# A decoder trunk in fp32 on one core: first weights of V split ahead of the scheduler, norm products two triples later, first output halves five blocks apart, late low weights by columns

## The chip, the cores and the metric

The kernel runs on one core of one Trainium2 chip. A core has TensorE (PE in the profile; its weight loads are listed as PEld), VectorE (DVE), ScalarE (ACT), GpSimd (POOL) and SyncE (SP, which here issues loads and stores). Each engine runs its own list of instructions in order, and waits by semaphores for the others. The metric is device time in microseconds (us) of one execution; lower is better.

## The reference

Two layers over 1024 positions of width 1024, all in fp32. The first is a gated delta rule with a gated FFN and was left as it is. The second is softmax attention over a band of keys, with a FFN behind it. The change lies between the end of the first FFN and the start of the second one:

```python
h = h + conv_ffn(rmsnorm(h, f_norm[0]), ...)              # layer 0 ends
kv = rmsnorm(h, kv_norm) @ w_kv                            # K and V, once
h = h + chunk_attention(rmsnorm(h, b_norm[0]), b_w_q[0], b_rel_bias[0], b_w_out[0], k_pad, v_pad)
# chunk_attention, for each chunk of 64 queries and each of 16 heads:
#   s = q . k * scale + bias          576 keys: own chunk and 8 before it
#   p = softmax(s);  o = p . v;       and at the end o @ w_out
h = h + conv_ffn(rmsnorm(h, f_norm[1]), ...)
```

## The kernel before

Every fp32 product is made of three matmuls of a faster type: an operand is split into a high part (a rounded copy: `whi`, `xh`, made on ACT) and a low part (the remainder: `wlo`, `xl`, made on POOL or DVE). `dense` (L114) then issues high × high (L120), high × low (L121) and low × high (L122). Three such matmuls, 128 × 128 by 128 × 512, are called a **block** here; the FFN's own form (L1395 to L1397) is called a triple. A tile of 128 output columns and all 1024 positions takes two halves `s` of 512 positions, each of 8 blocks, one for each 128 rows of the weights.

**End of the first FFN and the norm.** `part` (L1832) issues the triples of the last FFN product for half `s`, tile `m` and step `k`. At listed places it calls `next(norms[0])`, which runs the next piece of `norm_steps` (L351): squares on ACT, sums on DVE into `nacc` (L369), products with ones on PE (`pss`, L374), the root on ACT, then a broadcast by PE (`psb`, L387), from which DVE makes the normed activations (L392), ACT their high part (L395) and DVE or POOL their low part (L383).

**First tiles of K and Q.** `two_tiles` (L1337) runs one tile of K and one of Q, half by half. Their weights come by `load_w`, which folds the norm's gain in and splits (`split_w`, L91).

**Attention.** The eight pairs of heads `p` each need a tile of K, of Q and of V (`kv_tile`, L2004). From here a planner written in the kernel, `Flow` (L200), decides the order in which the code is emitted: it keeps a clock `T`, adds an assumed duration for all that it emits, holds a due time for each engine, and emits a dense block whenever nothing of higher rank is due. `Flow.fetch` prepares the next dense tile: a first step issues its load, a second splits its weights. If the tile at the front isn't split yet, `_dense` adds 3 us and more to the clock and then splits. Its order is fixed before the kernel runs. A tile of K or Q of pair `p` may start only when all scores of pair `p − 2` are out (`there`, key `scored`), because `kA` and `qA` have two buffers for each pair of tiles; one of V when the outputs of `p − 2` are.

For two heads and 256 queries at a time the attention goes as follows. PE writes scores to the one buffer `sc` (L2140, L2141). DVE adds the bias and takes the extreme into `sS` and `st` (L2145). ACT takes the exponential (L2149), DVE a reciprocal (L2153), POOL multiplies (L2155). PE transposes the result (`ptp`, L2200); ACT makes its high part `pTh` (L2213), DVE its low part `pTl` (L2220), and PE multiplies by V into `poT` (L2245, L2246). ACT and DVE fold that into `oT` (`tm` L2251, L2256). V itself is copied (`vt`, L2083), transposed on PE (`pvt`, L2064) and split into `V`.

**Output product.** `first_parts` (L2336) runs the first two tiles `m` of the output product over six of the eight weight rows, on activations made from `yo` (L2293 high, L2296 low). Its list `order` holds (m, s, k). `rest(s)` (L2381) adds the last two rows for half `s`, with weights in two pieces of 512 columns, and feeds the second FFN's norm.

Of the kernel before, what the change touches and what calls it, by code (L numbers as in the profile page):

```python
# [28 lines left out]
def trunk_kernel(  # L29
# [15 lines left out]
    nc = tc.nc  # L45
# [20 lines left out]
    g_kv = take(8)  # L66
    g_b = take(8)
# [334 lines left out]
    wv = None  # L402
# [107 lines left out]
    with ExitStack() as ph:  # L510
        wp = ph.enter_context(tc.tile_pool(name="wp0", bufs=2, **SB))
# [776 lines left out]
        wv = Flow()  # L1288
# [16 lines left out]
        with tc.manual_schedule(engines={mybir.EngineType.PE, mybir.EngineType.DVE, mybir.EngineType.Activation}):  # L1305
            tails = []
            acts, normed = [[[[None, None] for _ in range(KT)] for _ in range(2)] for _ in range(2)]
            for t in range(4):
                s, hds = heads(t)
# [24 lines left out]
            env["cut"] = 1  # L1334
            del env["run"]

    def two_tiles(wts, tail):  # L1337

        pss = [[pacc.tile([P, HALF], F32, name="acc", tag="u", bufs=4) for _ in range(2)] for _ in wts]
        for s in range(2):  # L1340
            for n, (ps, wt) in enumerate(zip(pss, wts)):
                for i in range(KT):
                    dense(ps[s], wt, 0, xh, xl, FULL[i : i + 1], s, first=i == 0, last=i == KT - 1)
                    if (n, i) in ((0, 6), (1, 3)):
                        next(tail, None)
            for _ in tail:
                pass
            yield pss
# [8 lines left out]
    def ffn(layer, h, hp, xs, tail, d_r, last):  # L1357
# [472 lines left out]
        if layer == 0:  # L1830

            def part(s, m, ks):  # L1832
                def f():
                    if ks[0] == 0:
                        if s == 0 and m > 3:
                            if m % 2 == 0:
                                fps["d"] = pacc.tile([P, SEQ], F32, name="pf", tag="d", bufs=2)
                            fps[s, m] = fps["d"][:, hs(m % 2)]
                        else:
                            fps[s, m] = pacc.tile([P, HALF], F32, name="pf", tag="u", bufs=4)  # L1840
                    for k in ks:
                        triple(fps[s, m], fw[m], [t_[:, hs(s)] for t_ in hid[k0 + k]], kc[k], k == 0, k == 3)
                        if (s, m, k) in ((1, 5, 1), (1, 6, 0)):
                            next(norms[0])
                return f

# [128 lines left out]
    ctx_o = ctx.enter_context(ExitStack())  # L1975
    wp = ctx_o.enter_context(tc.tile_pool(name="wp1", bufs=2, **SB))
    xh, xl = xb
    first = two_tiles([load_w(w_kv, 0, fold=g_kv, on_act=True), load_w(b_w_q, 0, fold=g_b, on_act=True)], tail0)
    next(first)
    ctx_f.close()  # L1980
    ctx_h.close()
# [2 lines left out]
    with ExitStack() as ph:  # L1984
# [18 lines left out]

        def kv_tile(src, c0, g, post):  # L2004

            shape = [P, KT, P]
            raw = wp.tile(shape, F32, name="wraw", tag="wraw", bufs=2)
            nc.sync.dma_start(out=raw, in_=src[:, c0 : c0 + P].rearrange("(k p) m -> p k m", p=P))
            yield
            wt = split_w(raw, shape, fold=g)  # L2010
            wv.on("G", 2.75, wv.on("A", 1.0, wv.on("G", 2.6)))
            yield
            for s in range(2):
                ps = pacc.tile([P, HALF], F32, name="acc", tag="acc", bufs=3)
                for i in range(KT):
                    dense(ps, wt, 0, xh, xl, FULL[i : i + 1], s, first=i == 0, last=i == KT - 1)
                    if i < KT - 1:
                        yield
                post(s, ps)
                yield  # L2020
# [291 lines left out]
        NO = 6  # L2312
# [23 lines left out]
        def first_parts():  # L2336
            raws = [part_raw(m) for m in range(2)]
            yield
            wts = [part_split(raws[0])]
            yield 20  # L2340
            wts.append(part_split(raws[1]))
            wv.brief = True
            order = [(0, 0, k) for k in range(3)]
            for k in range(3, NO):
                order += [(1, 0, k - 3), (0, 0, k)]
            order += [(1, 0, k) for k in range(NO - 3, NO)] + [(0, 1, k) for k in range(NO)]
            banks, done = {}, []
# [33 lines left out]
        def rest(s):  # L2381
            w_ = 1024 // (KT - NO)
            shape = [P, KT - NO, w_]
            raws, wts = [], []
            for c in range(KT - NO):
                raws.append(wp.tile(shape, F32, name="wraw", tag="wraw", bufs=2))
                nc.sync.dma_start(out=raws[c], in_=b_w_out[NO * P :, c * w_ : (c + 1) * w_].rearrange("(k p) m -> p k m", p=P))
            yield
            wts.append(split_w(raws[0], shape))
            wv.on("G", 2.7, wv.on("A", 1.0))  # L2390
            yield 11
            for m in range(KT):
                c = m * P // w_
                ps = pacc.tile([P, HALF], F32, name="acco", tag="acc", bufs=3)
                for k in range(NO, KT):
                    dense(ps, wts[c], m * P - c * w_, *acts, [(k - NO, k)], s, first=k == NO, last=k == KT - 1)
                    if k < KT - 1:
                        yield
                if m == 0:
                    wts.append(split_w(raws[1], shape))  # L2400
                    wv.on("G", 2.7, wv.on("A", 1.0))
# [19 lines left out]
                yield wv.T + (0.8, 2.2)[n] if n < 2 else wv.T + 1.1  # L2421

        queue_kv(0)
        wv.auto = False
        main_ps.close()
        pB = ph.enter_context(tc.tile_pool(name="pB", bufs=1, **PS))
        pacc = ph.enter_context(tc.tile_pool(name="paccB", bufs=1, **PS))
        env["cut"] = 4
        with tc.manual_schedule():
            for p in range(1, 8):  # L2430
                queue_kv(p)
            wv.add(1, "score", lambda: 0.0, score_run())
            wv.add(0.8, "turns", lambda: 0.0, turn_run())
            wv.add(0.6, "apply", lambda: 0.0, apply_run())
            for n, (s, k) in enumerate([(s, k) for s in range(2) for k in range(NO)]):
                wv.add(0.9, ("early", n % 6), wv.when(("d_o", k)), early_o(k, s))
            wv.add(0, "begin", wv.when(("o", 6), ("act", 6, 0), ("act", 6, 1)), begin())
            wv.dense.append((lambda: True, there(("act", 0, 0)), first_parts()))
            for m in range(2, KT):
                wv.dense.append((lambda: True, lambda: True, part(m, (0, 1) if m < 4 else (0,))))  # L2440
            for s in range(2):
                wv.dense.append((lambda: True, there(*[("act", k, s) for k in range(NO, KT)]), rest(s)))
                if s == 0:
                    for m in range(4, KT):
                        wv.dense.append((lambda: True, lambda: True, part(m, (1,))))
            wv.run(lambda: not (wv.dense or wv.items or wv.late or wv.cur or wv.nxt))
# [96 lines left out]
```

## Time and profile before

| | us |
|---|---|
| runs of the kernel, median (lowest to highest) | 2573.83 (2572.54 to 2575.70) |
| the profiled execution | 2573.15 |
| its span, first to last instruction | 2571.4 |
| first FFN ends, norm | about 1293 to 1340 |
| first tiles of K and Q | about 1340 to 1366 |
| attention | about 1366 to 1896, output product from 1775 |
| second FFN | from 1896 |

In the profile, a group's row gives the line, engine, operation, output and inputs by the program's names, and how many. Rows of the timeline begin with the start and the duration in us, and in brackets stands how long the engine was idle before and what released it. Rows of the waits give engine, tile and line, then what was waited for, and total us, times and longest us. Rows of the windows give for a stretch the length, the busy time of PE, PEld, DVE, ACT and POOL with the number of instructions in brackets, then the granted TensorE clock as a share of full speed, the busy share of the DMA engines and GB/s. L-numbers are lines of the kernel before.

### The profile page before, as it was taken

Reading aid. Unit: us, or ns where it says so; the run is one execution under the profiler, and the core shown is the slowest. Engines: PE = TensorE matmul, PEld = TensorE weight load, DVE = VectorE, ACT = ScalarE, POOL = GpSimd, SP = SyncE. Lnnn points to the kernel's source line nnn. Section 1 sums busy time; section 2 is a strip of 40 time slices with the busy share of each in tenths; the row PEclk is TensorE's granted clock in tenths of the full one; section 3 lists DMA queues with packets and bytes.
Section 4 is the critical chain, followed back from the end, with each engine's and each line's share of the span. In section 5 each row is a group of like instructions: output and inputs, shape, how many; then the busy total and the mean of one; then the engine's idle time right before and its main releaser. Section 6 shows DMA issues by size and latency. Waiting matters only on the chain. (4 is left out here: it accounts for less than half of the span.)

```text
span 2571.4 us, 39303 instructions
## 1 busy us (share of the span) xinstructions
PE 2506.2 (97%) x13957; PEld 2081.7 (81%) x13957; DVE 1824.8 (71%) x2956; ACT 1405.4 (55%) x2704; POOL 1484.8 (58%) x1511
## 2 busy tenths in 40 slices
PE   7999999999999999999999999999999999999998
PEld 5878788888777888888788888888877788888877
DVE  5765775454588888888866666666478788888885
ACT  6444555474456555565545555556455656555653
POOL 3655554245537777777725444445453777777770
PEclk9999999999999999999999999999999999999999
DMA  4534445455326676777841211122332467677785
GB/s 128 138 101 121 119 117 164 130 176 167 112 78 136 143 152 143 155 152 152 185 164 46 61 43 48 53 69 71 128 119 78 135 148 147 146 155 153 155 194 189
DMA packets 317061, 325.93 MB, mean 127 GB/s; under 512 B 32832, under 2 KB 240960, under 8 KB 316864
## 3 DMA queue, kind: packets, MB, share of 16 engines
q1 hardware_dynamic: 285728, 219.33, 28.7%
q0 software_dynamic: 26240, 95.43, 20.7%
q10 hardware_dynamic: 4896, 8.65, 1.0%
q8 instruction: 110, 1.80, 0.3%
q14 instruction: 87, 0.71, 0.1%
HBM read 180.68 MB, written 142.67 MB: 126 GB/s over the span
## 5 line engine op out<-in xcount | busy, mean ns | idle before, releaser
L1362 POOL TENSOR_TENSOR ul<-r,uh 128x512 fp32r<-128x512 f32 x276 | 438.3, 1607 | 276.1 <-ACT uh L1383 261.6
L105 POOL TENSOR_TENSOR wlo<-wraw,whi 128x256 fp32r<-128x256 f32 (+3 forms) x338 | 249.3, 768 | 227.1 <-ACT whi L103 192.4
L120 PE MATMUL acc<-xh,whi 128*128 128x512 f32 x896 | 377.8, 422 | 0.2
L122 PE MATMUL acc<-xh,wlo 128*128 128x512 f32 x896 | 354.9, 396 | 3.2 <-POOL wlo L105 3.2
L121 PE MATMUL acc<-xl,whi 128*128 128x512 f32 x896 | 355.1, 396 | 1.0 <-DVE xl L1102 0.6
L1383 ACT CAST uh<-r 128x512 fp32r<-128x512 f32 x290 | 178.2, 623 | 202.0 <-DVE r L1362 159.0
L1397 PE MATMUL pu<-xh,ul 128*128 128x512 f32 x528 | 207.1, 392 | 3.7 <-POOL ul L1362 3.7
L1395 PE MATMUL pu<-xh,uh 128*128 128x512 f32 x528 | 207.0, 392 | 2.9 <-POOL uh L1383 1.4
L1396 PE MATMUL pu<-xl,uh 128*128 128x512 f32 x528 | 206.5, 391 | 1.0 <-POOL xl L383 1.0
L122 PEld LDWEIGHTS acc<-xh,wlo 128*128 128x128 f32 x896 | 169.7, 189 | 41.4 <-POOL wlo L105 3.9
L1749 ACT COPY stage<-pd 128x1024 f32<-128x1024 f32 x180 | 174.9, 1013 | 50.3 <-PE pd L1397 49.4
L121 PEld LDWEIGHTS acc<-xl,whi 128*128 128x128 f32 x896 | 170.8, 191 | 27.3 <-DVE xl L1102 2.7
L120 PEld LDWEIGHTS acc<-xh,whi 128*128 128x128 f32 x896 | 170.7, 190 | 24.6 <-ACT xh L1101 1.1
L1490 DVE SCALAR_TENSOR_TENSOR gate<-gpre,colt,gate 128x1023 f32<-128x1023 f32 (+2 forms) x92 | 180.0, 1957 | 4.7 <-ACT gate L1487 3.8
L1362 POOL TENSOR_TENSOR dl<-a,dh 128x512 fp32r<-128x512 f32 x90 | 153.8, 1709 | 46.0 <-ACT dh L1383 46.0
L2155 POOL TENSOR_SCALAR sS<-sS,st 128x640 f32<-128x640 f32 (+4 forms) x128 | 85.7, 674 | 163.5 <-DVE st L2153 147.9
L1490 DVE SCALAR_TENSOR_TENSOR val<-vpre,colt,val 128x1023 f32<-128x1023 f32 x88 | 151.9, 1726 | 35.7 <-ACT val L1487 35.5
L2145 DVE CUSTOM_DVE_ANT_0 sS<-sc,bt 128x640 f32<-128x640 f32 (+4 forms) x128 | 84.1, 657 | 123.6 <-PE sc L2141 97.0
L1362 DVE TENSOR_TENSOR r<-r,r 128x512 f32<-128x512 f32 x160 | 126.4, 790 | 31.0 <-POOL ul L1362 29.6
L1397 PEld LDWEIGHTS pu<-xh,ul 128*128 128x128 f32 x528 | 99.5, 188 | 26.7 <-POOL ul L1362 6.2
L2213 ACT CAST pTh<-ptp 128x512 fp32r<-128x512 f32 (+2 forms) x176 | 76.1, 452 | 81.2 <-PE ptp L2200 79.6
L1395 PEld LDWEIGHTS pu<-xh,uh 128*128 128x128 f32 x528 | 99.4, 188 | 24.2 <-POOL uh L1383 1.9
(406 smaller groups left out, 7131.9 us busy)
## 6 DMA issues: line engine op xcount, KB each, us to landing
r<-in_f_w_up_dram SPq DMA_DIRECT2D x172, 256.0 KB, 4.3
d_r<-stage POOLq DMA_DIRECT2D x78, 512.0 KB, 7.7
d_c<-stage POOLq DMA_DIRECT2D x70, 512.0 KB, 7.8
a<-in_f_w_down_dram SPq DMA_DIRECT2D x72, 256.0 KB, 2.8
wraw<-in_a_w_in_dram SPq DMA_DIRECT2D x32, 512.0 KB, 4.7
d_e<-stage POOLq DMA_DIRECT2D x32, 512.0 KB, 8.8
wraw<-in_a_w_out_dram SPq DMA_DIRECT2D x16, 512.0 KB, 4.3
d_r<-h ACTq DMA_DIRECT2D x32, 256.0 KB, 3.4
```

The costliest lines, as they stand in the source:

```text
L105: nc.gpsimd.tensor_tensor(lo[:, c], raw[:, c], hi[:, c].bitcast(F32), op=ALU.subtract)
L120: mm(ps, hi[:, kw, wcol : wcol + P], rh[k][s], start=st, stop=False)
L121: mm(ps, hi[:, kw, wcol : wcol + P], rl[k][s], start=False, stop=False)
L122: mm(ps, lo[:, kw, wcol : wcol + P], rh[k][s], start=False, stop=sp)
L1362: tt = lambda eng, o, a, b, op: eng.tensor_tensor(o, a, b, op=op)
L1383: copy(hi, src)
L1395: mm(ps, w[0][:, cw], x[0], start=first, stop=False, skip_group_check=True)
L1396: mm(ps, w[0][:, cw], x[1], start=False, stop=False, skip_group_check=True)
L1397: mm(ps, w[1][:, cw], x[0], start=False, stop=last, skip_group_check=True)
L1490: nc.vector.scalar_tensor_tensor(t_[:, a:c1], p_[:, a - step : c1 - step], w[:, 2 - step : 3 - step], t_[:, a:c1], op0=ALU.mult, op1=ALU.add)
L1749: nc.scalar.copy(t_, ps)
L2155: nc.gpsimd.tensor_scalar(S, S, st[:, 3:4], 1.0, op0=ALU.mult, op1=ALU.mult)
```

## The change

1. In `two_tiles` a function `then` is called after K's second half. It issues the load and the split of V's first tile. `kv_tile` takes those weights if they are there. The next tile's load and split are asked for (`wv.fetch(0)`, `wv.fetch(2)`), and the first bias tiles are loaded, before the planner starts.
2. Two calls of the norm's steps move from the triples (1,5,1) and (1,6,0) to (1,5,3) and (1,6,2).
3. In `first_parts`, the first tile's half runs five blocks, not three, before the second tile's blocks alternate with it.
4. In `rest`, a weight piece's low part is made in four column groups of 128, over both its rows, instead of in one operation for each row.

```diff
-    def two_tiles(wts, tail):
+    def two_tiles(wts, tail, then):
...
+                if (s, n) == (1, 0):
+                    then()
...
-                        if (s, m, k) in ((1, 5, 1), (1, 6, 0)):
+                        if (s, m, k) in ((1,5,3),(1,6,2)):
                             next(norms[0])
...
+    ready = []
+
+    def next_tile():
+        raw = wp.tile([P, KT, P], F32, name="wraw", tag="wraw", bufs=2)
+        nc.sync.dma_start(out=raw, in_=w_kv[:, 1024 : 1024 + P].rearrange("(k p) m -> p k m", p=P))
+        ready.append(split_w(raw, [P, KT, P], fold=g_kv))
...
-            yield
-            wt = split_w(raw, shape, fold=g)
-            wv.on("G", 2.75, wv.on("A", 1.0, wv.on("G", 2.6)))
+            if ready:
+                wt = ready.pop()
+                yield
+            else:
...
-            order = [(0, 0, k) for k in range(3)]
-            for k in range(3, NO):
-                order += [(1, 0, k - 3), (0, 0, k)]
-            order += [(1, 0, k) for k in range(NO - 3, NO)] + [(0, 1, k) for k in range(NO)]
+            order = [(0, 0, k) for k in range(5)]
+            for k in range(5, NO):
+                order += [(1, 0, k - 5), (0, 0, k)]
+            order += [(1, 0, k) for k in range(NO - 5, NO)] + [(0, 1, k) for k in range(NO)]
...
+            def split(raw):
+                hi = wp.tile(shape, F32R, name="whi", tag="whi")
+                lo = wp.tile(shape, F32R, name="wlo", tag="wlo")
+                nc.scalar.copy(hi, raw)
+                for c in range(w_ // P):
+                    nc.gpsimd.tensor_tensor(lo[:, :, kc(c)], raw[:, :, kc(c)], hi[:, :, kc(c)].bitcast(F32), op=ALU.subtract)
...
         queue_kv(0)
+        wv.fetch(0)
+        wv.fetch(2)
...
         with tc.manual_schedule():
+            bias(0)
```

Since the planner's clock no longer stands at the opening, the order of the whole attention changes. Three places follow, first the opening of V's first tile on PE, before the change (`acc_13428` is V's first half, `sc` the scores):

```order
L120 MATMUL acc_13428<-xh0_0_13075,whi_13421 128x512
L121 MATMUL acc_13428<-xl0_0_13076,whi_13421 128x512
L122 MATMUL acc_13428<-xh0_0_13075,wlo_13422 128x512
L120 MATMUL acc_13428<-xh1_0_13077,whi_13421 128x512
L121 MATMUL acc_13428<-xl1_0_13078,whi_13421 128x512
L122 MATMUL acc_13428<-xh1_0_13077,wlo_13422 128x512
L2140 MATMUL sc_13446<-kA_13378,qA_13388 128x128
L2141 MATMUL sc_13446<-kA_13378,qL0_13390 128x128
```

After the change, all eight blocks of the first half (`acc_13436`) come first; these are the rows from its last block on:

```order
L120 MATMUL acc_13436<-xh7_0_13095,whi_13360 128x512
L121 MATMUL acc_13436<-xl7_0_13096,whi_13360 128x512
L122 MATMUL acc_13436<-xh7_0_13095,wlo_13361 128x512
L120 MATMUL acc_13467<-xh0_1_13241,whi_13360 128x512
L121 MATMUL acc_13467<-xl0_1_13242,whi_13360 128x512
L122 MATMUL acc_13467<-xh0_1_13241,wlo_13361 128x512
L2077 MATMUL pvt_13471<-ident_67,vt_13465 128x128 x4
...
L122 MATMUL acc_13467<-xh3_1_13247,wlo_13361 128x512
L2153 MATMUL sc_13501<-kA_13391,qA_13401 128x128
L2154 MATMUL sc_13501<-kA_13391,qL0_13403 128x128
```

So the first score stands behind 12 blocks of V where it stood behind two, and the first transposes of V (`pvt`) behind one block of the second half.

The second place is PE between V's fourth tile and K's fifth. Before (`acc_15416` is the end of that V tile, `acc_15530` that K tile):

```order
L122 MATMUL acc_15416<-xh7_1_13255,wlo_15203 128x512
L2200 MATMUL ptp_15510<-ident_67,sS_15289 128x128
L2200 MATMUL ptp_15510<-ident_67,sS_15342 128x128
...
L2245 MATMUL poT_15498<-pTh_15459,V_14718 128x256
L2246 MATMUL poT_15498<-pTl_15460,V_14718 128x256
...
L2064 MATMUL pvt_15523<-ident_67,vt_15506 128x128 x4
L120 MATMUL acc_15530<-xh0_0_13075,whi_15424 128x512
```

After, between the same two tiles (now `acc_15210` and `acc_15450`), one row for each group that stands there; a score has four such rows, a group of transposes two to four, a group of `poT` four:

```order
L122 MATMUL acc_15210<-xh7_1_13255,wlo_15062 128x512
...
L2077 MATMUL pvt_15325<-ident_67,vt_15305 128x128 x4
...
L2259 MATMUL poT_15333<-pTl_15322,V_14620 128x256
...
L2153 MATMUL sc_15350<-kA_14257,qA_14459 128x320
...
L2153 MATMUL sc_15370<-kA_14257,qA_14459 128x320
...
L2213 MATMUL ptp_15396<-ident_67,sS_15254 128x128
...
L2153 MATMUL sc_15405<-kA_14257,qA_14459 128x320
...
L2258 MATMUL poT_15413<-pTh_15363,V_14621 128x256
...
L2153 MATMUL sc_15426<-kA_14257,qA_14459 128x320
...
L2213 MATMUL ptp_15436<-ident_67,sS_15355 128x128
...
L2258 MATMUL poT_15444<-pTh_15391,V_14621 128x256
...
L120 MATMUL acc_15450<-xh0_0_13081,whi_15235 128x512
```

Where one group of transposes, one of `poT` and V's transposes stood, there are now four scores and the attention work between them, with no dense block.

The third place is the start of the output product on PE. Before, the second tile (`acco_18306`) follows the first (`acco_18272`) after three blocks:

```order
L122 MATMUL acco_18272<-xh2_0_18106,wlo_18149 128x512
L2200 MATMUL ptp_18297<-ident_67,sS_17950 128x128
L2200 MATMUL ptp_18297<-ident_67,sS_17994 128x128
...
L120 MATMUL acco_18306<-xh0_0_18102,whi_18265 128x512
L121 MATMUL acco_18306<-xl0_0_18103,whi_18265 128x512
L122 MATMUL acco_18306<-xh0_0_18102,wlo_18266 128x512
```

After, two more blocks and two scores with `poT` groups stand between the third block and the second tile (`acco_18294`):

```order
L122 MATMUL acco_18224<-xh2_0_18100,wlo_18113 128x512
L2077 MATMUL pvt_18243<-ident_67,vt_18196 128x128 x4
...
L122 MATMUL acco_18224<-xh3_0_18102,wlo_18113 128x512
...
L2153 MATMUL sc_18262<-kA_17592,qA_17857 128x128
...
L122 MATMUL acco_18224<-xh4_0_18104,wlo_18113 128x512
L2153 MATMUL sc_18282<-kA_17592,qA_17857 128x256
...
L122 MATMUL acco_18294<-xh0_0_18096,wlo_18218 128x512
```

On POOL the order at this place is the same in both, except that one product of scores (`sS`) moves ahead of the activations: three low parts of activations (`xl`), then the low part of the second weights.

More of the change, by code (lines that the diff above doesn't have):

```diff
@@ L1977, in trunk_kernel @@
     xh, xl = xb
-    first = two_tiles([load_w(w_kv, 0, fold=g_kv, on_act=True), load_w(b_w_q, 0, fold=g_b, on_act=True)], tail0)
+    ready = []
[3 more added lines that the diff above has]
+        ready.append(split_w(raw, [P, KT, P], fold=g_kv))
+    first = two_tiles([load_w(w_kv, 0, fold=g_kv, on_act=True), load_w(b_w_q, 0, fold=g_b, on_act=True)], tail0, next_tile)
     next(first)
@@ L2004, in kv_tile @@
         def kv_tile(src, c0, g, post):
-            shape = [P, KT, P]
-            raw = wp.tile(shape, F32, name="wraw", tag="wraw", bufs=2)
-            nc.sync.dma_start(out=raw, in_=src[:, c0 : c0 + P].rearrange("(k p) m -> p k m", p=P))
-            yield
-            wt = split_w(raw, shape, fold=g)
-            wv.on("G", 2.75, wv.on("A", 1.0, wv.on("G", 2.6)))
+            if ready:
+                wt = ready.pop()
+                yield
+            else:
+                shape = [P, KT, P]
+                raw = wp.tile(shape, F32, name="wraw", tag="wraw", bufs=2)
+                nc.sync.dma_start(out=raw, in_=src[:, c0 : c0 + P].rearrange("(k p) m -> p k m", p=P))
+                yield
+                wt = split_w(raw, shape, fold=g)
+                wv.on("G", 2.75, wv.on("A", 1.0, wv.on("G", 2.6)))
             yield
@@ L2388, in rest @@
             yield
-            wts.append(split_w(raws[0], shape))
-            wv.on("G", 2.7, wv.on("A", 1.0))
+            def split(raw):
[4 more added lines that the diff above has]
+                    nc.gpsimd.tensor_tensor(lo[:, :, kc(c)], raw[:, :, kc(c)], hi[:, :, kc(c)].bitcast(F32), op=ALU.subtract)
+                wv.on("G", 2.9, wv.on("A", 1.0))
+                wts.append((hi, lo))
+            kc = lambda c: slice(c * P, (c + 1) * P)
+            split(raws[0])
             yield 11
@@ L2399, in rest @@
                 if m == 0:
-                    wts.append(split_w(raws[1], shape))
-                    wv.on("G", 2.7, wv.on("A", 1.0))
+                    split(raws[1])
                 nc.vector.tensor_tensor(h[m][:, hs(s)], ps, h[m][:, hs(s)], op=ALU.add)
```

## The prediction

> **What bounds the kernel now.** I read the page first, for the share of each engine.
>
> ```profile
> span 2571.4 us, 39303 instructions
> PE 2506.2 (97%) x13957; PEld 2081.7 (81%) x13957; DVE 1824.8 (71%) x2956; ACT 1405.4 (55%) x2704; POOL 1484.8 (58%) x1511
> ```
>
> TensorE (PE) is the bound: in a span of 2571.4 us it has no matmul under way for only 65 us. No edit here removes a matmul, so the change can only touch those 65 us, and the speed at which matmuls run. Next I read the table of waits, which names what ended each idle time of PE. These are its rows on the code that the diff touches, or whose order it can move:
>
> ```profile
> PE acco L122 <- POOL wlo L105: 2.7, 3, 1.9
> PE sc L2140 <- DVE qL L2051: 2.3, 1, 2.3
> PE pvt L2064 <- ACT vt L2083: 0.9, 4, 0.3
> PE sc L2140 <- DVE st L2145: 0.8, 1, 0.8
> PE pss L374 <- DVE nacc L369: 0.6, 1, 0.6
> ```
>
> Together 7.3 us, 0.28% of the span. Then I read busy time and granted clock in short stretches, because the two longest of these waits are followed by something that the table doesn't show:
>
> ```profile
> 1370.00:1373.00 3.00, 3.00 (x11) 2.34 (x10) 0.73 (x4) 1.09 (x4) 0.00 (x0) 0.55 0.86 273
> 1373.00:1376.00 3.00, 3.00 (x14) 2.51 (x13) 0.71 (x4) 0.71 (x2) 0.83 (x2) 0.88 0.00 0
> 1780.00:1783.00 3.00, 3.00 (x12) 2.64 (x12) 1.78 (x4) 1.88 (x5) 3.00 (x6) 0.50 0.53 156
> 1783.00:1786.00 3.00, 3.00 (x14) 2.44 (x13) 0.37 (x2) 0.00 (x0) 3.00 (x3) 0.94 0.88 296
> 1893.00:1900.00 7.00, 4.43 (x19) 3.05 (x18) 6.69 (x10) 4.05 (x7) 6.27 (x5) 1.00 0.89 285
> ```
>
> The number behind POOL's busy time is the granted clock. It is 0.55 and then 0.88 behind the wait that ends at 1369.6, and 0.50 and then 0.94 behind the one that ends at 1779.8. PE counts as busy there, but does less. Lost in the first pair: 3 × 0.45 + 3 × 0.12 = 1.7 us; in the second: 3 × 0.50 + 3 × 0.06 = 1.7 us. In the last row PE is idle for 2.6 of 7 us and the clock stays 1.00, so idle time alone doesn't decide it.
>
> **Weights of V in front of the scheduler, first wait.** In the before, only two blocks of V's tile stand ahead of the first score, which waits for the low part of the query tile:
>
> ```profile
> 1366.90 0.40 PE L122 MATMUL acc<-xh,wlo 128*128 128x512 f32 x1
> 1368.07 1.39 DVE L2051 SCALAR_TENSOR_TENSOR qL<-acc,qA 64x512 fp32r<-64x512 f32 x2
> 1369.61 0.30 PE L2140 MATMUL sc<-kA,qA 128*128 128x128 f32 x1 [2.31 <-DVE qL L2051]
> ```
>
> After the change 12 blocks stand ahead of it (order of the change: 8 of the first half, 4 of the second). A block is three matmuls, and matmuls of 512 columns start 0.23 us apart though each is recorded with 0.39 or 0.40 (1882.50 and 1882.73 below); so a block is 0.68 us, and a recorded wait costs 0.16 us more than it says. The ten added blocks last 6.8 us, far more than the 2.31 us. Gain: 2.31 + 0.16 + 1.7 of clock = **4.2 us**; at least 2.5, if the clock drops there for another reason. Those blocks are brought forward, not added: they are missing later, which is the last term of the sum. V's casts and subtractions move ahead of the last casts of K and Q on ACT and POOL, and the load of the next K tile moves behind two bias loads on SP's queue; all three have some 6 us of V blocks more in front of them than before. The one new price: V's first transposes (pvt) now come one block after the copy they need. The row above has four such waits, 0.9 us together; a fifth is 0.2 + 0.16, about **0.4 us** lost (0 to 0.5).
>
> **Norm's products two triples later.**
>
> ```profile
> 1330.29 0.39 PE L1397 MATMUL pf<-hidh,fl 128*128 128x512 f32 x1
> 1331.30 1.05 PE L374 MATMUL pss<-ones,nacc 128*128 128x2 f32 x8 [0.63 <-DVE nacc L369]
> 1337.53 0.69 DVE L1362 TENSOR_TENSOR h<-pf,h 128x512 f32<-128x512 f32 x1 [1.31 <-PE pf L1397]
> ```
>
> Two triples are 1.4 us of matmuls put in front of a wait of 0.63. Gain 0.63 + 0.16 = **0.8 us**. The products themselves start 0.6 us later than now, and with them the root, the reciprocal and the broadcast behind them; VectorE idles 1.31 us before the next sum that it takes from PE, longer than 0.6, so I cost this at nothing. Without that cover up to 0.6 comes back: bounds 0.2 to 0.8.
>
> **Halves five blocks apart.** At the first output tiles PE stands for the low half of the second weights, which is behind three subtractions of activations on POOL:
>
> ```profile
> 1774.09 3.80 POOL L2296 TENSOR_TENSOR xl<-yo,xh 128x512 fp32r<-128x512 f32 x3
> 1779.27 2.00 POOL L105 TENSOR_TENSOR wlo<-wraw,whi 128x128 fp32r<-128x128 f32 x3
> 1779.77 0.68 PE L122 MATMUL acco<-xh,wlo 128*128 128x512 f32 x1 [1.89 <-POOL wlo L105]
> ```
>
> POOL's order around it stays (order: three xl, then these lows). On PE the second weights' first block now comes after five blocks, two score pairs, six transposes and two groups of poT instead of three blocks and four transposes: by the issue times used below 5.2 us of matmuls behind the tile's start instead of 2.4. The wait was 1.89 + 0.16 = 2.05, so 0.8 us are to spare if POOL is no later. Gain 2.05 + 1.7 of clock = **3.8 us**, bounds 0 (POOL's rows move later with it) to 3.8.
>
> **Late lows by columns.**
>
> ```profile
> 1882.30 2.52 POOL L105 TENSOR_TENSOR wlo<-wraw,whi 128x512 fp32r<-128x512 f32 x2 [0.72 <-ACT whi L103]
> 1882.50 0.40 PE L120 MATMUL acco<-xh,whi 128*128 128x512 f32 x1
> 1882.73 0.39 PE L121 MATMUL acco<-xl,whi 128*128 128x512 f32 x1
> 1883.63 0.50 PE L122 MATMUL acco<-xh,wlo 128*128 128x512 f32 x1 [0.51 <-POOL wlo L105]
> 1884.87 0.50 PE L122 MATMUL acco<-xh,wlo 128*128 128x512 f32 x1 [0.28 <-POOL wlo L105]
> L105 POOL TENSOR_TENSOR wlo<-wraw,whi x32: 455/738/1296, 1844.1 to 1887.3; 128x128 fp32r<-128x128 f32 x12, 128x256 fp32r<-128x256 f32 x12, 128x512 fp32r<-128x512 f32 x8
> 1893.57 1.62 POOL L383 TENSOR_TENSOR xl<-h,xh 128x512 fp32r<-128x512 f32 x1 [3.30 <-ACT xh L395]
> ```
>
> Now two pieces of 1.26 us, each needed by its own block; then four of 256 elements, for which the median form's 0.74 us is the nearest row, and the first serves both blocks. PE's third matmul was due at 1882.96 and ran at 1883.63; with the first low at 1882.30 + 0.74 + 0.06 = 1883.10 it waits 0.14. Removed: 0.67 + 0.44 − 0.14 = **1.0 us**. Eight half-size pieces cost POOL 8 × 0.74 against 4 × 1.26 for both halves of the row group, 0.9 us more, ahead of a place where it waits 3.30 us for activations. Without that cover the next tile's activations are later by up to 0.4: bounds 0.6 to 1.0. The earlier group (its first half of rows) has no wait of PE, and I cost it at nothing.
>
> **What the new order costs.** Ten blocks used early are missing where nothing else is at hand. In the order of the change the fifth K tile may not start before the third pair's last score, because kA has two buffers. Between V's fourth tile and that K tile PE then has 6.7 us of attention work alone, with four scores of 640 in it (order rows shown above). In the before, the same place holds 1.2 us. The longest place without a dense block that the trace does have is at 1790, some 2.4 us with two waits of 0.8 and 0.3. What the chain of a score and of its weights takes:
>
> ```profile
> 1527.35 0.31 PE L2140 MATMUL sc<-kA,qA 128*128 128x320 f32 x1
> 1527.93 0.28 PE L2245 MATMUL poT<-pTh,V 128*128 128x256 f32 x1
> 1528.24 0.82 DVE L2145 CUSTOM_DVE_ANT_0 sS<-sc,bt 128x640 f32<-128x640 f32 x1 [1.32 <-PE sc L2141]
> 1528.99 0.08 DVE L2145 DVE_READ_ACCUMULATOR2_ANT st<- 128x1 f32 x1
> 1793.50 0.08 DVE L2145 DVE_READ_ACCUMULATOR2_ANT st<- 128x1 f32 x1
> 1793.64 0.50 PE L2140 MATMUL sc<-kA,qA 128*128 128x512 f32 x1 [0.77 <-DVE st L2145]
> 1518.58 0.60 PE L2200 MATMUL ptp<-ident,sS 128*128 128x128 f32 x4
> 1519.27 0.59 ACT L2213 CAST pTh<-ptp 128x512 fp32r<-128x512 f32 x1 [0.40 <-PE ptp L2200]
> 1519.89 0.69 DVE L2220 TENSOR_TENSOR pTl<-ptp,pTh 128x512 fp32r<-128x512 f32 x1 [0.82 <-ACT pTh L2213]
> 1526.03 0.83 ACT L2149 ACTIVATE sS<-sS,st 128x640 f32<-128x640 f32 x1 [2.07 <-DVE st L2145]
> 1529.32 0.80 POOL L2155 TENSOR_SCALAR sS<-sS,st 128x640 f32<-128x640 f32 x1 [2.78 <-DVE st L2153]
> ```
>
> There is one score buffer. A score's issue is 1527.93 − 1527.35 = 0.58 us; its sum with the bias ends at 1529.07, 1.72 after its start; the next score starts 0.06 after such an end (1793.58 to 1793.64). So two scores can't be nearer than 1.78 us. In the stretch 0.26, 0.85 and 0.36 us of other PE work stand between them (a transpose at 0.09 us, a poT matmul of 256 columns at 0.12: the recorded 0.60 for four and 0.28, less the 0.25 and 0.16 that overlap what follows); missing 0.94, 0.35 and 0.84. VectorE is also busy with low parts when the fourth is due, 0.3 more. The two groups that need low parts (ptp start to pTl end: 2.0 us; 0.8 of work between, and a copy of 0.35 ahead on ACT) wait 0.85, the transposes of V 0.3, and the last transposes, behind cast, exponential (0.83), reciprocal and POOL's product (0.80), 0.48. The sum is 4.06: **4.1 us** lost. Scaling 1790 gives 1.06 × 6.7 / 2.4 = 3.0. The lower end is 2.1 (score buffer alone), the upper 6.8, if each of the six waits becomes as long as the longest, 1.14. I take 4.1, since each row lies beside this work.
>
> **Sum**: − 4.2 − 0.8 − 3.8 − 1.0 + 0.4 + 4.1 = **−5.3 us**. The profiled execution took 2573.15 us (span 2571.4): 2567.9. The median of the runs is 0.7 above it, so 2568.5.
>
> **Rivals.**
> - *The stretch falls to half clock too.* Its waits sum to 4 us in 11; the profile has half clock after 1.9, and none after two of 1.45 and 1.12 (the 7 us row). It would cost 1.7 more: −3.6, 2570.2. Chance 0.18.
> - *The clock drops for another reason* than these two waits, and stays half for 3.4 us near the same places. Then 1.7 is gained at neither: −1.9, 2571.9. The rows speak against it, since both drops stand right behind a wait. Chance 0.06. By the Trainium skill, "TensorE: Matmul & The Clock Gate", Part 1, the clock is halved after an idle window of about 3.4 us; by that rule waits of 2.3 and 1.9 us would be too short, and this rival's time would come out. The trace disagrees in the length: 1.89 us of wait stood ahead of half clock.
> - *The stretch is filled*, since its low parts are ready earlier than I count: 2.1 lost, −7.3, 2566.5. Chance 0.14.
> - *The five blocks don't suffice*: the spare is 0.8 us and POOL is shared with scores' products. The wait and its clock stay: 5.3 − 3.8, −1.5, 2572.3. Chance 0.13.
> - *Slower: scores in series.* If the order makes each score of the stretch wait for its own predecessor's whole chain, PE to VectorE to ACT to POOL and back (1.72 + 0.83 + 0.16 + 0.80 + 2.0 = 5.5 us), then the three later ones cost 3 × 5.5 − 2.3 (the work that lies between them) = 14 us instead of 4.1. It decides from 9.4 on, the sum of all gains less V's 0.4. Result +4.8, 2578.6. Six buffers of scores speak against it. Chance 0.06.
>
> Forecast 0.43. A measurement here can tell about 0.2%, 5.1 us, so faster by that is below 2568.7; the forecast lies on that edge, and I count 0.6 of it below. Faster: 0.26 + 0.14 + 0.03 of the first rival = 0.43; slower by that much 0.05 of the last one's 0.06; the same 0.52. The range takes in the filled stretch with all bounds good (2564.5) and the wait that stays with half clock (2574).
>
> **What would show it.** The changed trace should have no wait of PE at the first score, and clock 1.00 in the 6 us behind it; at the first output block no wait of 1.9 and clock 1.00; pss without a wait; the two late acco waits at 0.1 or none. Near 1525 there should be a new cluster of waits of sc, poT and ptp for DVE and POOL, 3 to 5 us in 11. If that cluster is 1 us, or its clock drops, my price of the order is wrong; if a wait stays at the first output block, the step on POOL is.

## The result, and the profile after

The changed kernel takes 2566.16 us (median; 2564.95 to 2567.86) where the kernel before takes 2573.57 beside it: a ratio of 0.9974, 95% interval 0.9964 to 0.9985. That is 7.4 us less. Measured once more later it was 2565.97 against 2570.25, ratio 0.9982 (0.9973 to 0.9990), 4.3 us less. The forecast was 2568.5, 5.3 us less, with a range of 2564.5 to 2574.

The table of PE's waits after the change; these rows answer to those shown of before:

```profile
PE sc L2153 <- DVE st L2158: 2.2, 3, 0.8
PE poT L2258 <- DVE oT L2269: 1.3, 3, 0.6
```

The first number is the total in us, then how many and the longest. The waits on `wlo` at the output product (2.7 us), on `qL` at the first score (2.3), of the transposes of V on `vt` (0.9) and of `pss` on `nacc` (0.6) are no longer in the table. Scores waiting for VectorE's `st` rose from one wait of 0.8 to three of 2.2 together, and three waits of `poT` are new. Where the two long waits stood, the windows of the changed kernel show full clock (the number behind POOL's busy time) and a PE with no idle time to speak of; the third window is the stretch between V's fourth tile and K's fifth:

```profile
1360.00:1372.00 12.00, 11.96 (x57) 9.60 (x56) 7.54 (x14) 6.05 (x10) 6.62 (x14) 1.00 0.30 89
1765.00:1780.00 15.00, 15.00 (x86) 12.85 (x85) 9.18 (x21) 9.49 (x24) 12.01 (x13) 1.00 0.68 217
1530.59:1541.35 10.76, 9.10 (x66) 7.84 (x65) 8.14 (x23) 7.42 (x20) 1.60 (x2) 1.00 0.00 0
```

The stretch is there as foretold, 10.76 us long, with PE idle for only 1.66 us of it by the records. Its timeline shows how much of a loss the records hide (start, duration, engine, operation, and in brackets the recorded idle time and its releaser):

```profile
1534.19 0.31 PE L2154 MATMUL sc<-kA,qL 128*128 128x320 f32 x1
1534.34 0.49 PE L2213 MATMUL ptp<-ident,sS 128*128 128x128 f32 x3
1534.65 0.82 DVE L2158 CUSTOM_DVE_ANT_0 sS<-sc,bt 128x640 f32<-128x640 f32 x1 [0.97 <-PE ptp L2213]
1535.40 0.08 DVE L2158 DVE_READ_ACCUMULATOR2_ANT st<- 128x1 f32 x1
1535.54 0.42 PE L2153 MATMUL sc<-kA,qA 128*128 128x320 f32 x1 [0.71 <-DVE st L2158]
...
1538.57 0.81 DVE L2158 CUSTOM_DVE_ANT_0 sS<-sc,bt 128x640 f32<-128x640 f32 x1
...
1539.31 0.08 DVE L2158 DVE_READ_ACCUMULATOR2_ANT st<- 128x1 f32 x1
...
1539.44 0.41 PE L2153 MATMUL sc<-kA,qA 128*128 128x320 f32 x1 [0.75 <-DVE st L2158]
```

A score starts 0.06 us after VectorE has finished with the one before it, as the step of the prediction said. But three transposes are recorded with 0.49 us and hold up the next matmul for only 0.26 by the prediction's count (in the kernel before, three of them start at 1528.40 and the next matmul at 1528.65). So of the wait from 1534.60 to 1535.54, 0.94 us by this estimate, the record says 0.71.

For the comparisons below I use one number of each trace: the time from the first block of K's first tile to the start of the last matmul of the output product. The same 3072 matmuls lie between these two in every kernel here (the count differs by one where an edge falls on a record), and nothing before or behind enters. For before and after:

```profile
1340.05:1894.52 554.47, 547.18 (x3072) 472.89 (x3071) 336.49 (x837) 309.00 (x703) 273.98 (x412) 0.99 0.22 67
```

```profile
1336.62:1885.39 548.77, 544.50 (x3072) 469.57 (x3071) 336.79 (x837) 310.99 (x702) 276.25 (x420) 1.00 0.22 69
```

This **part** is 5.7 us shorter. Of these, 3.4 are the two stretches of half clock that the prediction shows in the trace of before (1.7 each); none falls into the part after the change. The edits themselves are worth the other 2.3 there. The part leaves out the norm's products, which lie ahead of it.

### The profile page after: what moved, and what is told of

Same layout as the page of the kernel before. It is cut to its first block, busy times and chain, and to the rows that moved or that the text cites. A ratio compares the mean times of both kernels' runs of the same rounds, so it can differ in the third digit from the quotient of the medians.

```text
span 2563.6 us, 39323 instructions
## 1 busy us (share of the span) xinstructions
PE 2503.4 (98%) x13957; PEld 2078.3 (81%) x13957; DVE 1824.7 (71%) x2956; ACT 1408.2 (55%) x2704; POOL 1487.8 (58%) x1519
## 5 line engine op out<-in xcount | busy, mean ns | idle before, releaser
L105 POOL TENSOR_TENSOR wlo<-wraw,whi 128x256 fp32r<-128x256 f32 (+2 forms) x330 | 238.9, 756 | 199.0 <-ACT whi L103 178.9
L1398 PEld LDWEIGHTS pu<-xl,uh 128*128 128x128 f32 x528 | 99.4, 188 | 22.4 <-POOL xl L383 2.1
```

The source lines that it names most:

```text
L105: nc.gpsimd.tensor_tensor(lo[:, c], raw[:, c], hi[:, c].bitcast(F32), op=ALU.subtract)
L1398: mm(ps, w[0][:, cw], x[1], start=False, stop=False, skip_group_check=True)
```

## The experiments

**One edit alone, and one edit undone.** The first kernel has only the split of V's weights; the second has all but that; the third has all but the five blocks.

```diff
 e1_v_only: before, with two_tiles(..., next_tile), kv_tile's ready.pop(), wv.fetch(0), wv.fetch(2), bias(0)
 e2_no_v:   before, with the norm's steps, the five blocks and split() by columns
 e3_no_five: after, with
-            order = [(0, 0, k) for k in range(5)]
-            for k in range(5, NO):
-                order += [(1, 0, k - 5), (0, 0, k)]
+            order = [(0, 0, k) for k in range(3)]
+            for k in range(3, NO):
+                order += [(1, 0, k - 3), (0, 0, k)]
```

> The kernel before with V's first weights split ahead of the scheduler alone. Theory: the wait at the first score goes (2.3 us, with 0.16 of pipe and 1.7 of half clock behind it), and the stretch without a dense block between V's fourth and K's fifth tile costs about as much again: 6.7 us of matmuls in 10.8 us. The time is then within 2 us of the kernel before (2571.5 to 2575). Rival, the stretch's waits are free because they would have come elsewhere: 4 us faster, about 2569.5. In the trace: no wait at the first score, clock 1.00 behind it, and the stretch from V's last block to K's first 10 to 11 us long.

> The changed kernel without the split of V's weights: the other three edits alone. Theory: norm 0.8, five blocks 3.8 with the clock, columns 1.0, together 5.6 us faster than before (about 2568), no dense-free stretch, the wait of 2.3 at the first score back, and half clock behind it. Rival, half clock isn't caused by these waits: 2.2 us less gain from the five blocks and no drop behind the first score, about 2570.

> The changed kernel with the output halves three blocks apart as before. Theory: a wait for the low half of the second weights comes back at the first output blocks, 1 to 2 us, with half clock behind it if it is near 1.9: 1 to 3.8 us slower than the changed kernel (2567 to 2570). Rival, the new order of the attention has already moved POOL's rows so that three suffice: no wait, same time as the changed kernel (2566.2).

V's split alone gave 2569.47 us, ratio 0.9991 (0.9981 to 1.0000): 1.5 us less than the kernel before beside it (2570.99), within the 2 us that the theory allowed and hardly to be told from no change. That interval also takes in the rival's 4 us; the parts, below, decide. The other three edits without it gave 2565.88, ratio 0.9978 (0.9968 to 0.9988), 5.1 us, where 5.6 was expected. Undoing the five blocks gave 2564.25, ratio 0.9971 (0.9960 to 0.9981), so nothing was lost by it. There the rival held. The part took 550.11, 548.05 and 548.85 us; in order:

```profile
1337.04:1887.15 550.11, 545.05 (x3073) 469.41 (x3071) 336.78 (x837) 311.14 (x703) 274.29 (x412) 1.00 0.22 69
```

```profile
1337.58:1885.63 548.05, 543.42 (x3073) 470.13 (x3071) 336.72 (x838) 309.15 (x703) 276.66 (x420) 1.00 0.22 68
```

```profile
1336.35:1885.20 548.85, 544.59 (x3072) 469.51 (x3071) 336.75 (x838) 311.08 (x702) 276.47 (x420) 1.00 0.22 69
```

So with the three other edits in place, V's split makes the part 0.7 us longer (548.77 against 548.05). It takes away 2.5 us at the first score and 0.9 in V's transposes there, so its new order costs about 0.7 + 2.5 + 0.9 = 4.1 us. Alone it makes the part about 1 us shorter, once the 3.4 us of half clock are taken from before's 554.47, though it removes waits of 2.5, of 0.9 and, at the output product, of 2.05, which the theory hadn't counted. So the stretch isn't free, and the rival is out.

Why three blocks suffice once V's weights come early, POOL's rows of that run show, in its timeline:

```profile
1767.90 1.30 POOL L2309 TENSOR_TENSOR xl<-yo,xh 128x512 fp32r<-128x512 f32 x1
1769.15 1.58 POOL L105 TENSOR_TENSOR wlo<-wraw,whi 128x128 fp32r<-128x128 f32 x3
```

The first output block of that run starts at 1767.02, so POOL begins the second weights' lows 2.1 us behind it. Before the change it began 4.5 us behind (1779.27 against 1774.77). The product of scores that stood between has moved ahead of the activations. The two edits remove the same wait, and either does it alone: the run with V's split alone has no wait at the first output block either, with three blocks there too.

The run without V's split has the wait at the first score back, as it should; but look at the clock behind it:

```profile
1367.11 0.30 PE L2140 MATMUL sc<-kA,qA 128*128 128x128 f32 x1 [2.32 <-DVE qL L2051]
```

```profile
1367.11:1370.11 3.00, 3.00 (x16) 2.52 (x17) 1.04 (x5) 1.10 (x4) 0.00 (x0) 1.00 0.86 273
```

A wait of 2.32 us, and full clock; before, 2.31 and half clock. So the 1.7 us of clock that the prediction booked there isn't certain; what decides it, the next run but one shows.

**Six blocks in place of twelve.** If the stretch is the price of the ten blocks that were brought forward, fewer of them should keep the gain and not pay it. One line tells the planner an earlier time for the first pair's K and Q:

```diff
         wv.fetch(0)
         wv.fetch(2)
+        wv.time[("kq", 0)] = 3.0
```

> The changed kernel with one line more, which tells the planner that the first pair's K and Q are ready at 3.0 us, so that 6 blocks of V instead of 12 stand ahead of the first score. Its order has no dense-free stretch (longest 2.1 us). Theory: six blocks (4.1 us) still cover the wait of 2.3, and the stretch's 4.1 us are won: 2562 (2561 to 2564). Rival, the stretch's loss is only moved, since attention and its chain through VectorE are the bound there: 2566, same as the changed kernel. If six blocks are too few, a wait at the first score of up to 1 us shows.

It took 2560.80 us, ratio 0.9957 (0.9944 to 0.9969). The part:

```profile
1336.08:1881.75 545.67, 543.55 (x3073) 469.71 (x3071) 333.88 (x836) 311.37 (x702) 276.12 (x420) 1.00 0.22 70
```

That is 3.1 us less than with twelve. The first score comes without a wait, as the timeline shows (a block, then the score 0.23 us after its last matmul):

```profile
1365.47 0.39 PE L122 MATMUL acc<-xh,wlo 128*128 128x512 f32 x1
1365.70 0.22 PE L2153 MATMUL sc<-kA,qA 128*128 128x128 f32 x1
```

and scores wait for `st` only once, for 0.8 us, at the end of the attention.

**What the clock does behind a wait.** This kernel leaves out the reference's computation: it runs matmuls of 512 columns, lets PE wait for one sum on VectorE, and runs matmuls again, 80 times.

```diff
+    for N in (512, 1024, 1280, ..., 3072):
+        for r in range(8):
+            ps = busy(40 + 7 * (count % 5), wt)
+            nc.vector.tensor_copy(add[:, 0:P], ps[:, 0:P])
+            nc.vector.tensor_tensor(low[:, 0:N], big[:, 0:N], add[:, 0:N], op=ALU.add)
+            busy(30, low[:, 0:P])
```

> Not the reference's computation: 47 to 77 matmuls of 512 columns, a wait of TensorE for one VectorE sum, 30 matmuls, 80 times, with sums of 512 to 3072 elements (waits of about 1 to 3.7 us), eight of each. Theory: whether the clock falls to half behind a wait is decided by where the wait lies against a window that runs free, so the share of waits with half clock rises with their length: none of eight at 1 us, some at 1.8 to 2.5, nearly all at 3.4 and more. Rival, a fixed length decides: all eight of one length or none, with the edge between 1.5 and 1.9 us; the wait of 2.32 without a drop in the run without V's split speaks against it. In both cases half clock lasts 3.4 us.

In fact 40 to 68 matmuls stood ahead of a wait, after the 30 that followed the wait before it.

Of the eight waits of each length, so many were followed by half clock (matmuls that start 0.43 us apart; counted in the trace):

```
recorded wait, us   1.2  1.7  2.0  2.3  2.5  2.8  3.1  3.3  3.6  3.9
half clock, of 8     0    0    4    3    6    5    7    7    8    8
```

Two equal waits, one without and one with it:

```profile
380.76 1.61 PE L96 MATMUL ps<-rhs,wait 128*128 128x512 f32 x6 [2.00 <-DVE wait L106]
423.34 2.55 PE L96 MATMUL ps<-rhs,wait 128*128 128x512 f32 x7 [2.00 <-DVE wait L106]
```

Equal waits go both ways between 2.0 and 3.3 us, so a fixed length is out; the share rises with the length, as the theory had it. What tells them apart stands in the same trace, in its record of the granted clock. All 48 drops begin on one grid of 3.413 us: the time between any two beginnings is a whole number of steps of this length, to within 0.02 us. Here are steps of that grid: the one with the wait that ends at 423.34 and the two behind it, then the two over which the wait that ends at 380.76 is spread.

```profile
420.82:424.23 3.41, 1.41 (x7) 0.89 (x6) 1.78 (x2) 0.00 (x0) 0.00 (x0) 1.00 0.00 0
424.23:427.64 3.41, 3.41 (x10) 2.64 (x9) 0.00 (x0) 0.00 (x0) 0.00 (x0) 0.50 0.00 0
427.64:431.06 3.42, 3.42 (x16) 2.84 (x16) 0.00 (x0) 0.00 (x0) 0.00 (x0) 1.00 0.00 0
376.44:379.86 3.42, 2.32 (x11) 1.58 (x9) 1.03 (x2) 0.00 (x0) 0.00 (x0) 1.00 0.00 0
379.86:383.27 3.41, 2.51 (x11) 2.14 (x12) 0.75 (x1) 0.00 (x0) 0.00 (x0) 1.00 0.02 5
```

The first wait lies whole in one step, which leaves PE 2.00 us idle there; the next step runs at half clock from end to end, and the one behind it at full clock. The second wait is cut by an edge of the grid into 1.10 and 0.90, and no drop follows. This separates all 80: each of the 48 waits that put 2.00 us or more into one step was followed by a drop, none of the 32 that put at most 1.91 into one was. In 44 cases the drop lasted one step, 3.41 us, and in four two steps: there the step at half clock itself held 0.7 us or more of the wait (elsewhere 0.6 at most). A drop that begins behind the wait holds 8 matmuls, and so costs 8 × 0.2 = 1.6 to 1.7 us.

The traces of all the other kernels have such a grid too; where its edges lie against the start of the program differs from trace to trace. It also explains the two equal waits at the first score, here in their steps, first before (the wait and the step behind it), then the run without V's split:

```profile
1366.92:1370.33 3.41, 1.10 (x6) 0.70 (x5) 3.10 (x6) 1.35 (x2) 2.25 (x6) 1.00 0.12 31
1370.33:1373.74 3.41, 3.41 (x10) 2.70 (x10) 0.55 (x4) 1.09 (x4) 0.00 (x0) 0.50 0.69 224
```

```profile
1362.20:1365.61 3.41, 2.59 (x11) 1.61 (x9) 3.34 (x6) 2.72 (x4) 2.81 (x4) 1.00 0.00 0
1365.61:1369.03 3.42, 1.92 (x10) 1.62 (x11) 2.50 (x7) 0.72 (x4) 1.06 (x5) 1.00 0.49 146
```

Before, 2.31 us lie in one step; without V's split an edge cuts 2.32 into 0.82 and 1.50. So the length sets the share, and the place on the grid decides; since the edges shift from execution to execution, it remains chance for whoever plans. In these kernels, where several waits and small matmuls share a step, the border is less sharp than in the test: the 1.89 us of before were followed by half clock, and 1.94 us in pieces, in the step from 1991.55, were not. This is the theory's window that runs free.

The Trainium skill, "TensorE: Matmul & The Clock Gate", Part 1, says of its window that it runs free and lasts about 3.4 us; the traces agree, with 3.413. That page's table of states asks for an idle window as a whole, and this isn't borne out: 2.0 us of idle time in one was enough.

**Three and eight blocks, and six with three.** The same line with 0.9 and 4.4, and the line with 3.0 in the kernel with three output blocks:

> As the run with six blocks, but K and Q told ready at 0.9 us, so 3 blocks of V stand ahead of the first score. No dense-free stretch either. Theory: the wait of 2.3 is one block (0.7) shorter than in the kernel before, 1.6 us, and the rest is as with six blocks: 1.8 us slower than it, up to 3.5 if the clock falls. Rival, that the blocks ahead of the first score don't set that wait: no difference from six blocks.

> As the run with six blocks, but ready at 4.4 us, so 8 blocks stand ahead of the first score; longest place without a dense block 2.1 us. Theory: the wait is covered and there is no stretch, so the same time as six blocks within 0.5 us. Rival, each block brought forward costs its share of the stretch's 4 us later (10 blocks, 0.4 each): 0.8 us slower.

> The run with six blocks and with the output halves three blocks apart, as before. Theory: V's early weights move POOL's rows ahead of the first output block as they did in the run with three blocks apart, so no wait there: the same time as six blocks. Rival, it was the twelve blocks that moved them: a wait of about 2 us at the first output blocks.

Three blocks: 2565.32 us, ratio 0.9976 (0.9967 to 0.9986), with a wait at the first score and the part 2.2 us longer than with six:

```profile
1368.54 0.30 PE L2153 MATMUL sc<-kA,qA 128*128 128x128 f32 x1 [1.82 <-DVE qL L2064]
```

```profile
1339.08:1886.93 547.85, 543.90 (x3073) 469.84 (x3071) 333.80 (x838) 311.46 (x702) 275.39 (x420) 1.00 0.22 69
```

1.82 + 0.16 = 2.0 of the 2.2 is the wait itself (1.6 was expected for it), with no half clock behind it in this trace. The medians differ by more: 4.5 us, or 3.7 against the run with six and three below, which was measured beside it. Whether other executions fell to half clock at this wait, no trace shows. Eight blocks: 2563.78, ratio 0.9969 (0.9958 to 0.9981), slower than six by the time, but not in the part, which took 545.39:

```profile
1339.99:1885.38 545.39, 543.31 (x3072) 469.75 (x3071) 333.86 (x838) 311.39 (x703) 275.79 (x420) 1.00 0.22 70
```

The whole difference of its trace to that with six stands ahead of 1340 (3.9 us), where the code is the same: five steps of half clock lie there, and three in the other, which is 3.4 us. So this time was misleading, and both were measured again. Six with three output blocks apart: 2561.66, ratio 0.9963 (0.9950 to 0.9976), part 545.67 as with five. The five blocks are worth nothing in this order either.

**Side by side on one chip.**

> The changed kernel once more, beside the next two on one chip. Theory: 0.997 of the kernel before; from the first K block to the last output block 548.8 us in its trace if no wait there falls to half clock.

> Six blocks of V ahead of the first score, once more. Theory: 3 to 4 us less than the changed kernel beside it, since the 4.1 us of the dense-free stretch are gone, and 545.7 us from the first K block to the last output block. Rival: its first result lay low by chance of the clock early in the program (3 us between traces there), and the difference to the changed kernel is under 1.5 us.

> Eight blocks ahead of the first score, once more. Theory: the same as six within 1 us (its trace had 545.4 us in the same part, and lost its 3 us to six before the change's place). Rival: each block brought forward costs, 2 to 3 us slower than six.

The changed kernel took 2565.97, six blocks 2562.13, eight 2560.73, the kernel before 2570.25; ratios 0.9982 (0.9973 to 0.9990), 0.9962 (0.9948 to 0.9976) and 0.9959 (0.9946 to 0.9972). The part took 548.78, 545.92 and 545.62. So six and eight can't be told apart, and are 3.8 and 5.2 us faster than the changed kernel; the traces account for 2.9 and 3.2 of that.

## Why the prediction held, and which of its terms did not

The time lay in the range, 2.3 us from the forecast; in the second measurement the gain was 4.3 us where 5.3 was forecast. The waits that were named went, and the stretch that was named came. But the clock and V's transposes were mis-sized in opposite directions, and two edits each remove the same wait, so that the time came out this near is in part luck.

- **V's weights, first wait**, 2.5 of wait and 1.7 of clock: the wait is gone, as said. The clock's 1.7 was taken as certain. The profiled execution of before had it, the run without V's split didn't at the same wait, since an edge of the grid cut it, and the test gives 3 of 8 for that length. The term should have been 2.5 + 3/8 × 1.7 = 3.1. The lower bound of 2.5 was in the text, for another reason.
- **V's transposes**, 0.4 lost by a fifth wait: the size was wrong, and the sign. The four recorded waits, 0.9 together, went from the table, and none came.
- **Norm's products**, 0.8: the wait of 0.63 is gone at this place in every run with the edit, and stands in the run with V's split alone. No wait came in its place, so the step's cover held.
- **Five blocks**, 3.8: alone it does remove the wait and what may follow it, as the run without V's split shows: no wait at the first output block. In the changed kernel it is worth nothing, since V's split has moved POOL's lows 2.4 us ahead by then. The step that failed is "POOL's order around it stays", with the spare worked out from before's times: the one product of scores that moves ahead of the activations stood in the order of the change, took 1.45 us between them and the lows in the kernel before, and was counted at nothing; the other 0.9 are PE's later place beside POOL's rows. Booked once, as now, the sum is still right; it was the reason that was shared by two edits. Its 1.7 of clock is chance as well, with none of eight at 1.7 us and four at 2.0. The rival that five blocks don't suffice is out by the run without V's split.
- **Late lows**, 1.0: right. The changed kernel has four pieces in place of two, and PE's third matmul at 1875.06 where 1874.93 was due, 0.13 late; 0.14 was worked out. The part shows 1.3: it is 550.11 with V's split alone and 548.85 in the run with three blocks apart, and no other edit between these two lies in it.

```profile
1874.27 2.83 POOL L2408 TENSOR_TENSOR wlo<-wraw,whi 128x256 fp32r<-128x256 f32 x4 [0.72 <-ACT whi L2406]
1874.70 0.39 PE L121 MATMUL acco<-xl,whi 128*128 128x512 f32 x1
1875.06 0.50 PE L122 MATMUL acco<-xh,wlo 128*128 128x512 f32 x1
```

- **The new order**, 4.1 lost: the stretch lasted 10.76 us where 6.7 + 4.1 was forecast. Its price comes out in two ways. Taking the stretch away, with six or eight blocks, gains 2.9 to 3.4 in the part. Putting V's split into the run without it costs 4.1 beyond the waits that it removes, as worked out above; and before to after gives the same (2.5 + 2.05 + 1.0 + 0.9 removed, 2.3 gained without the clock: 4.2). So 4.1 holds as the price of the whole new order; why the orders with six and eight blocks win back only 3 of it isn't shown. The split into work and waits was a little off: the 6.7 counts a transpose at 0.09 wherever it stands, and four of them ahead of V's transposes took 0.46 here, not 0.35:

```profile
1530.99 0.62 PE L2213 MATMUL ptp<-ident,sS 128*128 128x128 f32 x4
1531.45 0.64 PE L2077 MATMUL pvt<-ident,vt 128*128 128x128 f32 x4
```

The places of the largest waits, before the second and the fourth score, were right (1535.54 and 1539.44 above). The cross-check at 1790 was misread: from 1790.51 to 1794.62 no dense block stands there, 4.1 us, so 3.0 of work beside the 1.06 of waits and not 2.4, and scaling it gives 2.3, not 3.0.

In sum: the clock was booked with 3.4 us and by the shares of the test is worth 0.6 to 1.5 on average (3/8 of 1.7, and up to 4/8 for the other wait). V's transposes stood some 1 us on the wrong side (0.4 lost; the 0.9 of before gained). These errors go against each other, and the sum by the corrected terms is 4 to 5 us, depending on whether the order is priced at 4.1 or 3.1. Both measured gains, 4.3 and 7.4, take that in by their intervals. What is left of that spread isn't explained by the place of the change.

How much two traces can differ in code that is the same, a wait at 312 shows:

```profile
PE acc L122 <- POOL wlo L105: 3.2, 1, 3.2
```

The wait of 3.2 us stands in both tables; before, the clock fell behind it (1.7 us). After, it didn't, since an edge of the grid at 310.45 cuts the wait into 1.5 and 1.7; but in that trace it fell at 1986.40, where before it didn't. So these two cancel. The two traces of the kernel with six blocks have three and seven steps of half clock before the end, and spans of 2558.6 and 2564.4 us. What a single trace shows of such a kernel carries several us of this chance.

Of the rivals, half clock in the stretch didn't come (clock 1.00 in its window), and neither did scores in series. The filled stretch, at 2.1, wasn't true either: 2.9 to 4.2 were lost. That the clock drops for another reason than the waits is out too: the waits bring it about, but only where one step of the grid holds enough of them.

## What to carry to other kernels

Work that fills a wait is taken from a later place: look in the new order for the longest stretch in which the engine that sets the time has nothing but a dependent chain, and work out that chain before booking the gain. Here half as many blocks filled the wait as well, and left no such stretch, for 3 us more. And two edits that each remove the same wait must not be added; undo one at a time.

## What the runs showed of the hardware

TensorE's granted clock changes only on a grid of 3.413 us, whose edges shift against the program from trace to trace. In the test, a step with 2.00 us or more of idle time was followed by a step at half clock (48 of 48 waits), and one with 1.91 or less was not (32 of 32). So waits far shorter than the step can cost 1.7 us beyond themselves: none of eight at 1.7 us did, about half at 2.0 to 2.3, all at 3.6 and more; and a wait of 3.2 us that an edge cuts into 1.5 and 1.7, at 312 in the changed kernel's trace, didn't. In a kernel of 2570 us with a handful of such waits this moves equal code by several us between two executions: seven steps of half clock against three went with 5.8 us more in the two traces of six blocks. And a recorded idle time of PE understates what a wait costs, by 0.16 us behind matmuls of 512 columns (recorded with 0.39, started 0.23 apart) and by an estimated 0.23 behind three transposes (recorded with 0.49, counted with 0.26); differences of starts don't.
